# 64-byte tiles ahead of the weight buffers, and the small tiles at the other end of SBUF

## The chip, the cores and the metric

The kernel runs on one core of a Trainium2 chip. The metric is the device time of one execution in microseconds (us). Engines: PE is TensorE, DVE is VectorE, ACT is ScalarE, POOL is GpSimd, SP is SyncE. The on-chip memory SBUF has 128 partitions. A tile takes the same range of bytes in each of its partitions, so "address" below means the byte at which a tile starts in every partition, and "at 32" means that this address leaves 32 when divided by 128.

## What is computed

Two transformer blocks are chained on one sequence of 256 tokens of width 1024, in fp32. Cut to what carries the time:

```
h = rmsnorm(x, g_mix);  proj = h @ w_in              # block 1
o_swa, o_dsa, o_mem = three attentions on slices of proj
merged = sum of gate_i * (o_i @ w_proj_i)
x = x + merged @ w_out
x = x + square(relu(rmsnorm(x) @ w_mlp_in)) @ w_mlp_out
h = rmsnorm(x, g_final)
for layer in 0, 1:                                    # block 2
    h = post_norm(h, 0.5 * (silu(h @ w1) * (h @ w3)) @ w2)
    mix = sgu(h) if layer == 0 else nsa(h)            # gated MLP / sparse attention
    h = post_norm(h, mix)
    h = post_norm(h, 0.5 * (silu(h @ w1') * (h @ w3')) @ w2')
```

Every weight matrix is used once, on all 256 tokens.

## The kernel before

**Weights.** All weights are streamed from HBM in strips of 128 x 1024 floats. `Stream.load` puts one into one of five raw buffers `wr` (SP's queue). `Stream.prep` splits it: ACT copies it, rounded, into a `wh` buffer (L142), DVE subtracts to get the remainder in a `wl` buffer (L149). In block 1's mixers there are six pairs of `wh` and `wl`; once block 1's tiles are released, `Stream.add` brings three more pairs (pools `whi2` and `wlo2`), and the nine are used in turn. In the program's listing the first six `wh` are called wh_69 to wh_79 and the three added ones wh_1996, wh_1998 and wh_2000.

**Products.** Activations are split the same way, so one product is three matmuls (`mm3`, L273: hi x hi, hi x lo, lo x hi). A matmul has one operand that is loaded into the array first (its weight load is the PEld row of the profile) and one that streams through it, the moving one. Three shapes of use carry nearly all of the time:

- `up` (L284): a strip of weights is loaded, the transposed activations (256 columns of a `big` or `med` tile) move. One half strip is 24 matmuls.
- `down` (L304, matmuls at L311): the hidden activations in `t2` tiles are loaded, the weights move in 512 columns. Chunks of 24. `down_last` (L313) does the end of it through `mm3`, in parts of 512 and 256 columns.
- `row` (L294): activations in `big` are loaded, the weights move in 512 or 256 columns.

**Where tiles lie.** `run` opens the pools one after the other, and each begins where the one ahead of it ends: raw, whi, wlo, cp (constants, vectors, rotary tables), bp (eight `big` of 8192 bytes), mp (five `med` of 4096 bytes), sm (scalars for each row). `blocks` then opens b1 and t2 for block 1's mixers, releases them, and opens t2 with eleven tiles, whi2, wlo2 and p2 for the rest. What this gives in the built program:

| tiles | address before | mod 128 | address after | mod 128 |
|---|---|---|---|---|
| wr, 5 | 1152 | 0 | 1152 | 0 |
| wh and wl, first 6 pairs | 21632 to 70784 | 0 | 21696 to 70848 | 64 |
| `big`, 8 | 72032 | 96 | 72064 | 0 |
| `med`, 5 | 137568 | 96 | 137600 | 0 |
| t2, 7 (mixers) | 187072 | 64 | 158080 | 0 |
| t2, 11 (the rest) | 161696 | 32 | 158080 | 0 |
| wh and wl, 3 more pairs | 184224 to 208800 | 32 | 180672 to 205248 | 64 |

Every one of these tiles is a multiple of 512 bytes long and is cut in multiples of 512 bytes, so where an operand starts modulo 128 is where its tile starts. The order of work on each engine is set by the build's scheduler, except for what `pin` and `manual` fix.

Of the kernel before, what the change touches and what calls it, by code (L numbers as in the profile page):

```python
# [23 lines left out]
F32 = mybir.dt.float32  # L24
F32R = mybir.dt.float32r
I32 = mybir.dt.int32
# [150 lines left out]
class Ker:  # L177
# [7 lines left out]
    def run(self, stop=None):  # L185
        self.stop = stop
        with ExitStack() as es:
            P = lambda n, b=1, **k: es.enter_context(self.pool(n, b, **k))
            self.W = Stream(self.nc, P("raw"), P("whi"), P("wlo"), self.specs, self.pin)
            self.cp = P("cp")  # L190
            self.bp = P("bp", 8)
            self.mp = P("mp", 5)
            self.sm = P("sm", 6)
            self.ps = P("ps", 4, space=bass.MemoryType.PSUM)
            self.dp = P("dp", space=bass.MemoryType.DRAM)
            self.blocks()
        return self.W.specs
# [345 lines left out]

    def rope_tables(self, p, pos):
        nc = self.nc
        posf = p.tile([128, 2], F32, name="posf")
        self.pin(nc.vector.tensor_copy(posf, pos))
        r = p.tile([128, 2, 32], F32, name="ang")
        q = p.tile([128, 2, 32], F32, name="angq")
        for t in range(2):  # L550
            nc.vector.tensor_scalar(r[:, t], self.cst("inv"), posf[:, t:t + 1], None, op0=OP.mult)
        magic = 12582912.0
        nc.vector.tensor_scalar(q, r, 1.0 / (2 * math.pi), magic, op0=OP.mult, op1=OP.add)
        nc.vector.tensor_scalar(q, q, magic, None, op0=OP.subtract)
        c1 = 6.28125
        c2 = float((np.array(2 * math.pi - c1, np.float32).view(np.int32) & ~np.int32(0xfff)).view(np.float32))
        c3 = float(np.float32(2 * math.pi - c1 - c2))
        for c in (c1, c2, c3):
            nc.vector.scalar_tensor_tensor(r, q, -c, r, op0=OP.mult, op1=OP.add)
        pif = 3.1415925  # L560
        nc.vector.tensor_scalar(r, r, pif, -pif, op0=OP.min, op1=OP.max)
        cosT = p.tile([128, 2, 64], F32, name="cosT")
        sinT = p.tile([128, 2, 64], F32, name="sinT")
        nc.scalar.activation(sinT[:, :, 32:64], r, AF.Sin)
        nc.scalar.activation(q, r, AF.Abs)
        nc.vector.tensor_scalar(q, q, -1.0, math.pi / 2, op0=OP.mult, op1=OP.add)
        nc.scalar.activation(cosT[:, :, 0:32], q, AF.Sin)
        nc.vector.tensor_copy(cosT[:, :, 32:64], cosT[:, :, 0:32])
        nc.vector.tensor_scalar(sinT[:, :, 0:32], sinT[:, :, 32:64], -1.0, None, op0=OP.mult)
        return cosT, sinT  # L570
# [178 lines left out]
    def blocks(self):  # L749
        nc, I = self.nc, self.I  # L750
        with ExitStack() as es:
            p = es.enter_context(self.pool("b1"))
            self.tp = es.enter_context(self.pool("t2", 7))
            R, merge = self.mixers(p)
        es = ExitStack()
        with es:
            self.tp = es.enter_context(self.pool("t2", 11))
            self.W.add(es.enter_context(self.pool("whi2")), es.enter_context(self.pool("wlo2")), 3)
            self.p2 = es.enter_context(self.pool("p2"))
            self.chain(R, merge)  # L760
# [215 lines left out]
    def toeplitz(self):  # L976

        nc, I = self.nc, self.I
        rel = self.p2.tile([32, 16], F32, name="rel")
        nc.scalar.dma_start(rel, I["rel_table_2"])  # L980
        hot = self.med([128, 384])
        self.load_cst(("hot",), hot)
        ps = self.bank()
        nc.tensor.matmul(ps[:16, :384], rel, hot[:32], start=True, stop=True)
        f = self.med([16, 384])
        nc.vector.memset(f[:, 256:], BIG)
        nc.vector.tensor_scalar(f[:, :256], ps[:16, :256], -1.0, None, op0=OP.mult)
        scr = self.dp.tile([16, 384], F32, name="scr")
        nc.scalar.dma_start(scr, f)
        out = []  # L990
        for i in range(2):
            tp = self.big([128, 8, 256])
            if not self.dry:
                src = bass.AP(tensor=scr.tensor, offset=scr.offset + i * 8 * 384, ap=[[1, 128], [384, 8], [1, 256]])
                nc.scalar.dma_start(tp, src)
            out.append(tp)
        return out

    def kv_ffn(self, x, acc):
# [69 lines left out]
        def windows(slot):  # L1069
            T = Ts[slot]  # L1070
            flt = self.med([128, 16, 4, 15])
            if self.dry:
                src = Null()
            else:
                t0 = T[:]
                src = bass.AP(tensor=t0.tensor, offset=t0.offset, ap=[list(t0.ap[0]), [2, 16], [S, 4], [16, 15]])
            pes = pe[:, slot, :, None, None].to_broadcast([128, 16, 4, 15])
            nc.vector.tensor_add(flt, src, pes)
            f = flt.rearrange("p j g n -> p j (g n)")
            nc.vector.memset(fl[slot][:, :, 60:64].bitcast(F32), 0.0)  # L1080
            self.split(fl[slot][:, :, :60], fl[slot][:, :, 64:124], f)

        def compress():
            hid = []
            for s in range(2):
                w1 = I["cmp_w1_2"][s]
                ws = W.get(w1, 0, 8, 0, 256) + W.get(w1, 1024, 8, 0, 256)
                ps = self.bank()
                k = 0
                for wh, wl in ws:  # L1090
                    for i in range(4):
                        f = fl[s][:, k]
                        ops = [(124, wh), (60, wl)]
                        for m, w in ops[::-1] if k == 15 else ops:
                            nc.tensor.matmul(ps[:m, :256], f[:, :m], w[:, i], start=k == 0 and m == 124,
                                             stop=k == 15 and m == 124, skip_group_check=True)
                        k += 1
                r = self.t2([128, 256])
                nc.vector.tensor_copy(r[:124], ps[:124, :256])
                ps = self.bank()  # L1100
                h = self.p2.tile([128, 2, 60], F32, name=f"hid{s}")
                for f in range(2):
                    nc.tensor.matmul(ps[:, f * 60:(f + 1) * 60], r[:124, f * 128:(f + 1) * 128], self.two[:124, :60],
                                     start=True, stop=True)
                for f in range(2):
                    nc.scalar.activation(h[:, f], ps[:, f * 60:(f + 1) * 60], AF.Gelu, bias=self.col("cmp_b1_2", 2 * s + f))
                hid.append(h)
# [21 lines left out]
            for r in range(4):  # L1129
                rs = slice(32 * r, 32 * r + 32)  # L1130
                nc.vector.tensor_copy(self.vc[rs, :, r], ps[rs, :256].rearrange("p (g d) -> p g d", g=4))

        f = self.ffn(x, 1, 0, acc, {1: keys, 2: lambda: windows(0), 3: lambda: windows(1), 4: lambda: key(0), 5: compress, 6: lambda: key(1)})
        for _ in range(3):
            next(f)
# [163 lines left out]
    def mixers(self, p):  # L1299
# [5 lines left out]
        self.c, self.vec, self.vt = {}, {}, []  # L1305
        nc.sync.dma_start(R[:, 0], I["x"][0, :128])
        names = ("ident", "tril_t", "rowok")
        self.load_cst(names, self.cp.tile([128, 257], F32, name="cst"))
        self.ident = self.cst("ident")
        put = [self.vectors(("g_mix", "g_mem"), nc.scalar)]  # L1310
        nc.sync.dma_start(R[:, 1], I["x"][0, 128:])
# [1 line left out]
            for _ in range(4):  # L1313
                W.load()
        self.load_cst(("swa", "causal", "inv"), p.tile([128, 800], F32, name="cstp"))
        pos = p.tile([128, 2], I32, name="pos")
        nc.scalar.dma_start(pos, I["positions"].rearrange("o (t p) -> p (o t)", p=128))
        nr = [self.med([128, D]) for _ in range(2)]
        put.append(self.vectors(("b_gate", "cmp_b1_2"), nc.sync))
# [28 lines left out]
        W.pump()  # L1348
        mem = self.big([128, 2, D])
        nc.sync.dma_start(mem, I["mem"][0].rearrange("(t p) d -> p t d", p=128))  # L1350
        sink = p.tile([128, 8], F32, name="sink")
        nc.scalar.dma_start(sink, I["sinks"].to_broadcast([128, 8]))
        nsink = p.tile([128, 8], F32, name="nsink")
        self.pin(nc.vector.tensor_scalar(nsink, sink, -1.0, None, op0=OP.mult))
        self.cosT, self.sinT = self.rope_tables(p, pos)

# [35 lines left out]
        nc.scalar.copy(vd, PI[:, :, 64:128])  # L1392
        dup = p.tile([128, 2, 2, 64], F32, name="kidup")
        nc.scalar.copy(dup, Ri[:, :, None, 256:320].to_broadcast([128, 2, 2, 64]))
        wi = p.tile([128, 2, 4], F32, name="wi")
        nc.vector.tensor_scalar(wi, PI[:, :, 448:452], 1.0 / 16, None, op0=OP.mult)
        kd = p.tile([128, 2, 64], F32, name="kd")
        self.rope(PI, 0, 1, kd, self.med([128, 2, 64]))
# [184 lines left out]
```

## Time and profile before

| | us |
|---|---|
| time, median of three runs | 1486.18 |
| the three runs, lowest and highest | 1483.34, 1486.90 |
| the profiled execution's own time | 1484.42 |
| its span, first to last instruction | 1482.6 |

The profile is of one execution; the mean granted clock of the PE in it is 0.997 of full speed. A matmul's duration in the profile is the time from its start to a modelled end and overlaps the next one: most 256-column matmuls read 282 ns. What back-to-back matmuls take is read instead from the length of a stretch divided by the number of matmuls that start in it; below this is called the pitch. The count behind a stretch's busy time also takes in the one or two matmuls that run on into it.

### The profile page before, as it was taken

What the parts mean: (1) busy time and instruction counts of PE and PEld (TensorE: products, weight loads), DVE (VectorE), ACT (ScalarE), POOL (GpSimd) and SP (SyncE); (2) the same over time, 40 slices, a digit from 0 to 9 for tenths busy, and PEclk for the clock granted to TensorE, in tenths of its full rate; (3) what the DMA queues carried; (4) which work ended last, traced back from release to release, by engine and by line L of the source; (5) the groups of instructions that cost most, each with busy time, mean ns of one, the idle gap of its engine ahead of it and who ended that gap; (6) DMA issues with size and microseconds to landing.
All of it is one profiled execution on the core that took longest, in us unless ns stands there. A gap on an engine that the chain in (4) does not pass through costs nothing.

```text
span 1482.6 us, 25196 instructions
## 1 busy us (share of the span) xinstructions
PE 1443.6 (97%) x10093; PEld 1330.6 (90%) x10093; DVE 954.6 (64%) x1618; ACT 734.1 (50%) x1115; POOL 40.1 (3%) x49
## 2 busy tenths in 40 slices
PE   7899999999999999999999999999999999999997
PEld 6689998989999999889899999999999898899996
DVE  7884488555585455886685454874665778664544
ACT  5564565544354444454354444454654397354442
POOL 0000000000000000100010000100000121100001
PEclk9999999999999999999999999999999999999999
DMA  8453267756556666487546666467665452286650
GB/s 292 129 157 93 65 225 242 223 187 189 171 171 201 192 189 187 138 264 266 157 156 213 186 185 189 134 219 229 219 208 183 125 180 86 67 260 187 185 170 29
DMA packets 191714, 264.81 MB, mean 179 GB/s; under 512 B 11024, under 2 KB 159852, under 8 KB 191596
## 3 DMA queue, kind: packets, MB, share of 16 engines
q1 hardware_dynamic: 183068, 249.56, 53.7%
q10 hardware_dynamic: 8528, 13.64, 3.0%
q8 instruction: 79, 1.29, 0.3%
q14 instruction: 39, 0.32, 0.1%
HBM read 262.09 MB, written 1.07 MB: 177 GB/s over the span
## 4 chain that ended last, share of the span: by engine, by line
PE 83%; DVE 9%; ACT 3%; DMA 2%; issue 2%; DVEq 0%; ACTq 0%
PE acc L311 21%; PE u L275 17%; PE u L276 17%; PE u L277 17%; DVE wl L149 2%; PE acc L695 2%; PE acc L276 1%; PE acc L277 1%; PE acc L275 1%; ACT wh L142 1%; DVE big L850 1%; PE acc L681 1%; DVE bst L379 1%; DMA wr<-in_w_in_dram 1%; DVE big L828 1%
## 5 line engine op out<-in xcount | busy, mean ns | idle before, releaser
L149 DVE TENSOR_TENSOR wl<-wr,wh 128x1024 fp32r<-128x1024 f32 (+3 forms) x488 | 572.6, 1183 | 419.5 <-ACT wh L142 410.6
L142 ACT CAST wh<-wr 128x1024 fp32r<-128x1024 f32 (+3 forms) x488 | 493.3, 1019 | 536.3 <-PE u L276 231.2
L275 PE MATMUL u<-big,wh 128*128 128x256 f32 x1960 | 552.1, 282 | 1.6 <-ACT med L412 1.1
L277 PE MATMUL u<-big,wl 128*128 128x256 f32 x1960 | 550.3, 281 | 0.0
L276 PE MATMUL u<-big,wh 128*128 128x256 f32 x1960 | 550.2, 281 | 0.0
L275 PEld LDWEIGHTS u<-big,wh 128*128 128x128 f32 x1960 | 369.7, 189 | 4.7 <-ACT med L412 1.3
L276 PEld LDWEIGHTS u<-big,wh 128*128 128x128 f32 x1960 | 368.9, 188 | 2.1
L277 PEld LDWEIGHTS u<-big,wl 128*128 128x128 f32 x1960 | 369.6, 189 | 0.0
L311 PE MATMUL acc<-wh,t 128*128 128x512 f32 x928 | 264.0, 395 | 0.0
L311 PEld LDWEIGHTS acc<-wh,t 128*128 128x128 f32 x928 | 169.8, 188 | 35.0
L311 PE MATMUL acc<-wl,t 128*128 128x512 f32 x464 | 145.6, 394 | 0.0
L311 PEld LDWEIGHTS acc<-wl,t 128*128 128x128 f32 x464 | 87.2, 188 | 20.6
L275 PE MATMUL u<-wh,big 128*128 128x256 f32 (+1 forms) x304 | 100.8, 332 | 0.5 <-ACT t L1423 0.5
L277 PE MATMUL u<-wh,big 128*128 128x256 f32 (+1 forms) x304 | 100.5, 331 | 0.0
L276 PE MATMUL u<-wl,big 128*128 128x256 f32 (+1 forms) x304 | 100.0, 329 | 0.0
L331 ACT CAST t<-t 128x512 fp32r<-128x512 f32 x66 | 41.0, 621 | 56.6 <-DVE t L536 25.3
L275 PEld LDWEIGHTS u<-wh,big 128*128 128x128 f32 x304 | 57.1, 188 | 6.9 <-ACT t L1423 0.9
L277 PEld LDWEIGHTS u<-wh,big 128*128 128x128 f32 x304 | 57.1, 188 | 5.5
L276 PEld LDWEIGHTS u<-wl,big 128*128 128x128 f32 x304 | 57.1, 188 | 5.2
L836 POOL TENSOR_TENSOR big<-big,med 128x256 f32<-128x256 f32 x24 | 23.2, 985 | 1384.6 <-ACT big L835 1352.1
L332 DVE TENSOR_TENSOR t<-t,t 128x512 fp32r<-128x512 f32 x66 | 45.3, 686 | 15.1 <-ACT t L331 15.1
L276 PE MATMUL acc<-wl,t 128*128 128x512 f32 (+1 forms) x168 | 53.9, 321 | 0.3 <-DVE wl L149 0.3
(256 smaller groups left out, 1344.3 us busy)
## 6 DMA issues: line engine op xcount, KB each, us to landing
wr<-in_ffn_w_dram SPq DMA_DIRECT2D x264, 512.0 KB, 4.4
wr<-in_w_in_dram SPq DMA_DIRECT2D x34, 512.0 KB, 4.5
wr<-in_w_mlp_in_dram SPq DMA_DIRECT2D x32, 512.0 KB, 4.6
wr<-in_w_mlp_out_dram SPq DMA_DIRECT2D x32, 512.0 KB, 3.9
wr<-in_sgu_w_in_dram SPq DMA_DIRECT2D x32, 512.0 KB, 5.3
wr<-in_sgu_w_out_dram SPq DMA_DIRECT2D x16, 512.0 KB, 5.5
wr<-in_kv_w_dram SPq DMA_DIRECT2D x12, 512.0 KB, 4.4
wr<-in_w_out_dram SPq DMA_DIRECT2D x8, 512.0 KB, 3.8
```

Of the source, the lines that this page charges most:

```text
L142: self.nc.scalar.copy(h, v)
L149: self.nc.vector.tensor_sub(l, v, h.bitcast(F32))
L275: mm(out, lh, rh, start=start, stop=False, **k)
L276: mm(out, lh, rl, start=False, stop=False, **k)
L277: mm(out, ll, rh, start=False, stop=stop, **k)
L311: mm(acc[t][n], a[:, k, ts], b[:, 0, n * 512:(n + 1) * 512], start=s, stop=e)
L331: self.nc.scalar.copy(h, x)
L332: return self.nc.vector.tensor_sub(l, x, h.bitcast(F32))
L379: b = nc.vector.bn_stats(st[:, 6 * i:6 * i + 6], x[:, c0:c1])
L681: nc.tensor.transpose(pt[:, c:c + 128], e[:, c:c + 128], self.ident)
L695: nc.tensor.matmul(out, PT[:, c:c + 128], v(b), start=b == 0, stop=b == nb - 1)
L836: nc.gpsimd.tensor_mul(x[:, cs], x[:, cs], gB[:, cs])
```

## The change

The pools are laid out anew, with nothing else edited in what is computed. A pool `sa` with one tile of 64 bytes (the positions as floats) stands between raw and whi, `sb` with one of 64 bytes (the sinks) behind wlo, and `sc` with one of 64 bytes (`rel`, the relative bias table) ahead of whi2. cp and sm are put at the other end of SBUF (`side="right"`), t2 of the mixers comes ahead of b1, and two tiles are padded (the constants from 257 to 288 floats, `hid` from 60 to 64 columns). The table above has the addresses. Before, the starts of the loaded and of the moving operand differed by 96 or 64 modulo 128 in `up`, by 32 or 64 in `row`, by 96 or 0 in `down`; after, weights start at 64 and activations at 0 in all three, in both parts of the program.

```diff
--- before.py
+++ after.py
@@ -186,11 +186,16 @@
         self.stop = stop
         with ExitStack() as es:
             P = lambda n, b=1, **k: es.enter_context(self.pool(n, b, **k))
-            self.W = Stream(self.nc, P("raw"), P("whi"), P("wlo"), self.specs, self.pin)
-            self.cp = P("cp")
+            raw, self.sa = P("raw"), P("sa")
+            posf = self.sa.tile([128, 16], F32, name="posf")
+            self.W = Stream(self.nc, raw, P("whi"), P("wlo"), self.specs, self.pin)
+            self.sb = P("sb")
+            self.posf, self.sink = posf, self.sb.tile([128, 16], F32, name="sink")
+            self.kp = P("kp")
+            self.cp = P("cp", side="right")
             self.bp = P("bp", 8)
             self.mp = P("mp", 5)
-            self.sm = P("sm", 6)
+            self.sm = P("sm", 6, side="right")
             self.ps = P("ps", 4, space=bass.MemoryType.PSUM)
             self.dp = P("dp", space=bass.MemoryType.DRAM)
             self.blocks()
@@ -543,7 +548,7 @@
 
     def rope_tables(self, p, pos):
         nc = self.nc
-        posf = p.tile([128, 2], F32, name="posf")
+        posf = self.posf[:, :2]
         self.pin(nc.vector.tensor_copy(posf, pos))
         r = p.tile([128, 2, 32], F32, name="ang")
         q = p.tile([128, 2, 32], F32, name="angq")
@@ -749,12 +754,13 @@
     def blocks(self):
         nc, I = self.nc, self.I
         with ExitStack() as es:
+            self.tp = es.enter_context(self.pool("t2", 7))
             p = es.enter_context(self.pool("b1"))
-            self.tp = es.enter_context(self.pool("t2", 7))
             R, merge = self.mixers(p)
         es = ExitStack()
         with es:
             self.tp = es.enter_context(self.pool("t2", 11))
+            self.rel = es.enter_context(self.pool("sc")).tile([128, 16], F32, name="rel")
             self.W.add(es.enter_context(self.pool("whi2")), es.enter_context(self.pool("wlo2")), 3)
             self.p2 = es.enter_context(self.pool("p2"))
             self.chain(R, merge)
@@ -976,7 +982,7 @@
     def toeplitz(self):
 
         nc, I = self.nc, self.I
-        rel = self.p2.tile([32, 16], F32, name="rel")
+        rel = self.rel[:32]
         nc.scalar.dma_start(rel, I["rel_table_2"])
         hot = self.med([128, 384])
         self.load_cst(("hot",), hot)
@@ -1098,7 +1104,7 @@
                 r = self.t2([128, 256])
                 nc.vector.tensor_copy(r[:124], ps[:124, :256])
                 ps = self.bank()
-                h = self.p2.tile([128, 2, 60], F32, name=f"hid{s}")
+                h = self.p2.tile([128, 2, 64], F32, name=f"hid{s}")[:, :, :60]
                 for f in range(2):
                     nc.tensor.matmul(ps[:, f * 60:(f + 1) * 60], r[:124, f * 128:(f + 1) * 128], self.two[:124, :60],
                                      start=True, stop=True)
@@ -1305,7 +1311,7 @@
         self.c, self.vec, self.vt = {}, {}, []
         nc.sync.dma_start(R[:, 0], I["x"][0, :128])
         names = ("ident", "tril_t", "rowok")
-        self.load_cst(names, self.cp.tile([128, 257], F32, name="cst"))
+        self.load_cst(names, self.kp.tile([128, 288], F32, name="cst"))
         self.ident = self.cst("ident")
         put = [self.vectors(("g_mix", "g_mem"), nc.scalar)]
         nc.sync.dma_start(R[:, 1], I["x"][0, 128:])
@@ -1313,7 +1319,7 @@
             for _ in range(4):
                 W.load()
         self.load_cst(("swa", "causal", "inv"), p.tile([128, 800], F32, name="cstp"))
-        pos = p.tile([128, 2], I32, name="pos")
+        pos = self.cp.tile([128, 2], I32, name="pos")
         nc.scalar.dma_start(pos, I["positions"].rearrange("o (t p) -> p (o t)", p=128))
         nr = [self.med([128, D]) for _ in range(2)]
         put.append(self.vectors(("b_gate", "cmp_b1_2"), nc.sync))
@@ -1348,9 +1354,9 @@
         W.pump()
         mem = self.big([128, 2, D])
         nc.sync.dma_start(mem, I["mem"][0].rearrange("(t p) d -> p t d", p=128))
-        sink = p.tile([128, 8], F32, name="sink")
+        sink = self.sink[:, :8]
         nc.scalar.dma_start(sink, I["sinks"].to_broadcast([128, 8]))
-        nsink = p.tile([128, 8], F32, name="nsink")
+        nsink = self.cp.tile([128, 8], F32, name="nsink")
         self.pin(nc.vector.tensor_scalar(nsink, sink, -1.0, None, op0=OP.mult))
         self.cosT, self.sinT = self.rope_tables(p, pos)
 
@@ -1392,7 +1398,7 @@
         nc.scalar.copy(vd, PI[:, :, 64:128])
         dup = p.tile([128, 2, 2, 64], F32, name="kidup")
         nc.scalar.copy(dup, Ri[:, :, None, 256:320].to_broadcast([128, 2, 2, 64]))
-        wi = p.tile([128, 2, 4], F32, name="wi")
+        wi = self.cp.tile([128, 2, 4], F32, name="wi")
         nc.vector.tensor_scalar(wi, PI[:, :, 448:452], 1.0 / 16, None, op0=OP.mult)
         kd = p.tile([128, 2, 64], F32, name="kd")
         self.rope(PI, 0, 1, kd, self.med([128, 2, 64]))
```

PE, POOL and SP run the same rows in the same order as before. On ACT the DMA that fetches the table `rel` (32 x 16 floats) stands at another place. Before, at the program's start, ahead of the first cast of a weight strip:

```order
L267 COPY vt_111<-u 128x16
L980 DMA rel<-in_rel_table_dram 32x16
L142 CAST wh_69<-wr_64 128x904
L142 CAST wh_71<-wr_65 128x904
L412 ACTIVATE med<-u,vt_111 128x128 x4
```

After, the first cast follows the copy, and the DMA is issued some 130 rows later, where the added buffers are first filled:

```order
L142 CAST wh_2009<-wr_72 128x256
L142 CAST wh_2011<-wr_68 128x256
L1540 ACTIVATE big<-big 128x512
L732 CAST med<-u 128x2x128
L142 CAST wh_2013<-wr_69 128x256
L986 DMA rel<-in_rel_table_dram 32x16
L142 CAST wh_81<-wr_72 128x512
L142 CAST wh_83<-wr_68 128x256
```

(wh_2009, wh_2011 and wh_2013 are the three added buffers there, wh_73 to wh_83 the first six.) The same place on ACT before:

```order
L727 CAST med<-u 128x2x128
L142 CAST wh_1996<-wr_68 128x256
L142 CAST wh_1998<-wr_64 128x256
L1534 ACTIVATE big<-big 128x512
L142 CAST wh_2000<-wr_65 128x256
L142 CAST wh_77<-wr_68 128x512
```

So besides the DMA, the last cast of an attention output (L727, L732 after; `rows_T`) has moved behind two casts of weights and one sigmoid step, and its partner on DVE behind the matching subtractions.

## Rows read from the trace of the kernel before

**Rows 1.** The page: busy time and share of each engine; granted clock in 40 slices.

```profile
PE 1443.6 (97%) x10093; PEld 1330.6 (90%) x10093; DVE 954.6 (64%) x1618; ACT 734.1 (50%) x1115; POOL 40.1 (3%) x49
PEclk9999999999999999999999999999999999999999
```

**Rows 2.** Stretch, length; busy (x) of PE, PEld, DVE, ACT, POOL; clock, DMA, GB/s.

```profile
205.00:250.00 45.00, 44.66 (x254) 37.30 (x253) 41.32 (x75) 24.85 (x34) 0.00 (x0) 1.00 0.69 234
250.00:430.00 180.00, 179.56 (x1174) 163.27 (x1173) 111.33 (x141) 85.41 (x102) 0.00 (x0) 1.00 0.59 186
430.00:600.00 170.00, 170.00 (x1215) 159.67 (x1215) 91.94 (x98) 75.43 (x83) 2.05 (x2) 1.00 0.63 195
```

**Rows 3.** Waits: who waited for whom, us in total, times, longest.

```profile
DVE wl L149 <- ACT wh L142: 410.6, 271, 5.4
ACT wh L142 <- PE u L276: 231.2, 168, 4.8
ACT wh L142 <- PE acc L311: 140.3, 98, 8.8
...
PE u L266 <- DMA med<-in_g_mem_dram: 6.3, 1, 6.3
```

**Rows 4.** Groups by line and form, whole span: count, busy, mean ns of one.

```profile
L149 DVE TENSOR_TENSOR wl<-wr,wh 128x1024 fp32r<-128x1024 f32 x458 | 556.3, 1223 | 405.6 <-ACT wh L142 396.7 <-PE u L276 6.6
L275 PE MATMUL u<-big,wh 128*128 128x256 f32 x1952 | 549.9, 282 | 1.6 <-ACT med L412 1.1 <-DVE nm L671 0.5
L142 ACT CAST wh<-wr 128x1024 fp32r<-128x1024 f32 x458 | 478.2, 1051 | 520.7 <-PE u L276 222.6 <-PE acc L311 140.3 <-issue 97.2
L311 PE MATMUL acc<-wh,t 128*128 128x512 f32 x928 | 264.0, 395 | 0.0
L311 PE MATMUL acc<-wl,t 128*128 128x512 f32 x464 | 145.6, 394 | 0.0
L275 PE MATMUL u<-wh,big 128*128 128x512 f32 x128 | 51.2, 400 | 0.5 <-ACT t L1423 0.5
L275 PE MATMUL u<-wh,big 128*128 128x256 f32 x176 | 49.6, 282 | 0.0
```

**Rows 5.** Stretches of `up` (128x256, `big` moving); columns as in Rows 2.

```profile
434.44:439.88 5.44, 5.44 (x50) 5.44 (x49) 4.27 (x4) 4.18 (x5) 0.00 (x0) 1.00 0.97 355
445.47:456.83 11.36, 11.36 (x97) 11.35 (x96) 5.04 (x5) 4.70 (x5) 0.00 (x0) 1.00 0.75 231
484.89:490.54 5.65, 5.65 (x50) 5.65 (x49) 2.45 (x3) 2.60 (x3) 0.00 (x0) 1.00 0.61 187
```

**Rows 6.** Chain of work, 428 to 510 us: start, length, `down` chunks of 24.

```profile
440.05 5.59 PE acc L311 x24
456.99 5.44 PE acc L311 x24
473.78 5.60 PE acc L311 x24
```

**Rows 7.** Stretches of `row` (weights moving), then of `down_last`; columns as in Rows 2.

```profile
622.44:623.84 1.40, 1.40 (x7) 1.12 (x6) 1.30 (x2) 0.00 (x0) 0.00 (x0) 1.00 0.98 342
640.57:643.32 2.75, 2.75 (x14) 2.25 (x12) 2.52 (x3) 2.33 (x4) 0.00 (x0) 1.00 0.97 306
757.23:758.59 1.36, 1.36 (x14) 1.36 (x13) 0.71 (x2) 1.36 (x3) 0.00 (x0) 1.00 0.00 0
759.96:762.76 2.80, 2.80 (x26) 2.80 (x25) 2.00 (x3) 2.79 (x5) 0.00 (x0) 1.00 0.69 204
232.26:232.98 0.72, 0.72 (x9) 0.72 (x7) 0.72 (x2) 0.00 (x0) 0.00 (x0) 1.00 0.35 114
```

**Rows 8.** Timeline of ACT: start, length, work, [idle before and its releaser].

```profile
6.62 0.33 ACTq L980 DMA_DIRECT2D rel<-in_rel_table_dram  x1
8.38 0.94 ACT L142 CAST wh<-wr 128x904 fp32r<-128x904 f32 x1 [1.59 <-DMA wr<-in_w_in_dram]
...
179.80 0.37 ACT L727 CAST med<-u 128x256 fp32r<-128x256 f32 x1 [0.85 <-PE u L724]
180.07 0.71 ACT L142 CAST wh<-wr 128x256 fp32r<-128x256 f32 x2
180.69 0.63 ACT L1534 ACTIVATE big<-big 128x512 f32<-128x512 f32 x1
181.22 0.39 ACT L142 CAST wh<-wr 128x256 fp32r<-128x256 f32 x1
183.65 0.62 ACT L142 CAST wh<-wr 128x512 fp32r<-128x512 f32 x1 [2.04 <-DMA wr<-in_w_proj_swa_dram]
```

## The prediction

> **What bounds the kernel now.** I read the page first: the PE is busy for 97% of the span, DVE for 64%, ACT for 50%, at a granted clock of 0.9 or more in every slice [rows 1] and 1.00 in the stages read here. Then the stages: through the long feed-forward stretches the PE has next to no gap, 179.56 of 180 us and 170.00 of 170, while DVE stands at 62% and 54% and the DMA engines at about 0.6 [rows 2]. The waits say the same from the other side. ACT's casts wait for the PE to give a weight buffer back (231 and 140 us), DVE's subtractions wait for the casts (411 us), and the PE's own largest wait is 6.3 us, once, at the start [rows 3]. So the time is the sum of what the matmuls take one after another, and a change that moves no work can change it only through that, or through a new gap.
>
> The grouped rows say that a 256-column matmul lasts 282 ns and a 512-column one some 395 to 400 [rows 4]. These are pipelined durations and don't sum to the span; what counts is the pitch, and it isn't the same everywhere. In `up`, 96 matmuls with weights in the first six buffers take 11.36 us, 118.3 ns each; 48 with weights in the three added buffers take 5.44 us, 113.3 ns; and 48 on the very same added buffers, 50 us later, take 5.65 us, 117.7 ns [rows 5]. In `down`, a chunk of 24 takes 5.59 or 5.60 us (233 ns) on the first six and 5.44 us (226.7 ns) on the added ones, a chunk with both in between [rows 6]. In `row` at 512 columns it is 1.40 us for six, 233.3 ns, on a buffer of the first six and 2.75 us for twelve, 229.2 ns, on added ones; at 256 columns 2.80 us for 24, 116.7 ns, against 1.36 us for twelve, 113.3 ns [rows 7]. Clock and shape are equal in these pairs, and the DMA share is not what tells them apart: 0.97 in the quickest stretch of `up`, 0.75 and 0.61 in the slower ones [rows 5]. What differs is which buffer is read, and with it the start modulo 128 of the two operands.
>
> Sorting all 6,060 matmuls of `up` by buffer, with their starts taken in order from the trace: the 4,242 on the first six (weights at 0, activations at 96) keep the 118.3 of the 445 us stretch throughout. The 1,818 on the added ones (at 32 and 96) have two levels, as the two short stretches show. 666 of them lie in half strips at about 113.3, 1,152 in half strips at about 117.8; the mean is 0.37 x 113.3 + 0.63 x 117.8 = 116.2. A level, once taken, mostly lasts until other buffers come.
>
> **The change, part by part.** The first part is the starts. After it, weights start at 64 and activations at 0, a difference of 64 for every pair. Today 64 is the difference of `up` and `row` on the added buffers, which is the better class of both, so I price the change by giving those pitches to all.
>
> - `up`, first six: 4,242 x (118.3 - 116.2) = 8.9 us less. Bounds: 0 (nothing moves) and 4,242 x 5.0 = 21.2 us (all at 113.3). I take the mean of the added buffers, since it has the new difference; that all would be at the lower level has only a third of that class for it.
> - `up`, added: difference 64 before and after, 0. Bounds: 1,818 x 2.9 = 5.3 us less, 1,818 x 2.1 = 3.8 us more.
> - `down`, first six, 1,038 matmuls at 512 columns with a difference of 96: no `down` of today has 64, so it takes the pitch of `row` at 64, 229.2 [rows 7]: 1,038 x (233.3 - 229.2) = 4.3 us less. Bounds 0 and 1,038 x 6.6 = 6.9 us.
> - `down`, added, 522 matmuls: difference 0 becomes 64. Their mean today is 228.8 (226.7 at best, [rows 6], more where a chunk mixes both kinds), so 522 x 0.4 = 0.2 us more. Bounds 1.1 less, 522 x 4.5 = 2.3 more.
> - `row` on the first six: 324 at 512 columns x 4.1 = 1.3 us less; 504 at 256 columns. Their new pitch is the mean of the 136 on added buffers, 115.9 (the 113.3 of rows 7 is their lower level): 504 x 0.8 = 0.4 us less. Bounds 0 and 2.1 + 1.7 us.
> - `down_last` at 256 columns, 335 matmuls at some 118.5: with both operands at 32 it reads 0.72 us for six, 120.0 [rows 7]. Taken as 0, bounds 1.7 less, 0.5 more.
>
> These lie on the path: back-to-back PE work ends each of these stretches, and the strips that feed it have slack (ACT's casts wait for the PE to free a buffer). The one stretch where that is thin is 205 to 250 us, with DVE at 41.3 of 45 us; there at most 0.5 us of the gain could turn into a wait.
>
> The second part is the moved rows. The DMA of `rel` takes 0.33 us of ACT's queue at 6.62 us, and the cast behind it waits until 8.38 us for its strip anyway [rows 8]: nothing is gained by its leaving. At its new place the same 0.33 us stands ahead of casts that wait 2.04 us for a strip at 183.65 us, so nothing is lost. The delayed cast L727 stands behind 0.71 us of casts and a 0.63 us sigmoid step; its result goes to a projection whose strip comes later. I take 0, bounds 0 and 1 us more. The third part, small tiles at the far end and padding, changes where ACT and DVE read. Their large rows show a single duration for all buffers, 1,223 and 1,051 ns a strip [rows 4], and both engines have slack: 0.
>
> Sum: 8.9 + 4.3 - 0.2 + 1.3 + 0.4 = 14.7 us. The profiled execution's 1484.42 would become 1469.7; the median of the runs is 1.8 us above it, so 1486.2 - 14.7 = 1471.5.
>
> **A rule weighed.** The rows show 113.3 to 118.3 ns at 256 columns, depending on buffers [rows 5]. The Trainium skill, "TensorE: Matmul & The Clock Gate", section "Step-by-step: what each phase is for", says that the PE reads moving operand and weights through two independent ports, and that loading the next weights doesn't steal bandwidth from the running matmul; addresses don't appear in it. By that rule this change does nothing, which is the second rival below. The trace doesn't settle it outright, but a pitch that differs by 4% with the same shape and clock speaks against it.
>
> **The rivals.**
>
> 1. All pairs at the lower level. If starts at 0 and 64 let every matmul run at 113.3 or 226.7, the bounds add up: 21.2 + 5.3 + 6.9 + 1.1 + 2.4 (`row`, 512) + 2.1 (`row`, 256) + 1.7 = 40.7 us, giving 1445. For it: every start then leaves 0 or 64, and in none of today's pairs do both (activations are at 96 or 32), so today's two levels may be what a start at 32 costs; and a lower level lasts once taken, with no buffer of the first kind left to break it. Against it: difference 64 today gives the upper level more often, and 512-column `row` at 64 has 229.2, not 226.7.
> 2. The start modulo 128 isn't the cause, but the region of SBUF (the first six lie at 21 to 71 KB, the added ones at 184 to 209 KB) or the order of work. Then nothing moves: 1486. For it: in today's trace start and region always change together. Against it: the same added buffers read two levels.
> 3. Slower: the pairs never take the lower level. Then `up` on the added buffers rises to 118.3 (3.8 us), `down` there to 233.3 (2.3 us), `row` at 512 by 132 x 4.1 = 0.5 us and at 256 by 0.1 us: 6.7 us more, 1493. For it: difference 0, which gives `down` its 226.7, exists no longer, and the upper level is the commoner one at 64. It decides as soon as `up` on the first six stays above 118.0. The worst pitch of the trace, 120.0 for all of `up` [rows 7], would add 4,242 x 1.7 + 1,818 x 3.8 = 14.1 us in place of the 3.8, 1503.
>
> **How the numbers follow.** A measurement of this kernel can tell about 0.3% (4.5 us) from no change. My forecast, a mixture of levels as today's difference of 64 shows it: 0.43. Rival 1: 0.24. Rival 2: 0.18. Rival 3: 0.15. The first two are faster by more than 0.3%, so faster 0.67, same 0.18, slower 0.15. The predicted time is the forecast's, 1471. Its own range, from half the sum to one and a half times it (7 to 22 us less), is 1464 to 1479. The range for all reaches from rival 1, 1445, to 1490, so that it leaves out most of rival 3 (0.12) and the far end of rival 1 (0.04).
>
> **What would show it.** Right: `up` on the first six buffers between 113.3 and 118 ns, with half strips at two levels; chunks of `down` near 5.5 us in place of 5.60; PE still at 97%, and all stages shorter by about 1% alike. Rival 1 shows 48 matmuls of `up` in 5.44 us everywhere. Rival 2 shows 11.36 and 5.60 unchanged. Rival 3 shows no stretch of `up` at 5.44 for 48 any more. The forecast is wrong too if a new wait of the PE shows near 184 us, or if casts and subtractions change their durations with the new addresses.

## The result and the profile after

The changed kernel takes 1461.81 us (median of four runs, 1461.58 to 1463.18) against 1484.91 us for the kernel before on the same chip: a ratio of 0.9846, 95% interval 0.9829 to 0.9863, or 23.1 us less. The prediction said 1471, in a range of 1445 to 1490; its forecast alone said 1464 to 1479.

The page of the changed kernel has nearly the same shares as [rows 1], with the PE still the engine that is always busy; its busy time fell by 23.8 us.

```profile
PE 1419.8 (97%) x10093; PEld 1311.5 (90%) x10093; DVE 955.1 (65%) x1618; ACT 733.8 (50%) x1115; POOL 40.2 (3%) x49
```

The waits, answering to [rows 3]: ACT and DVE wait for the same things as before, in these two rows 20 and 24 us less in all, as they would if the PE gives buffers back sooner.

```profile
DVE wl L149 <- ACT wh L142: 386.4, 213, 5.1
ACT wh L142 <- PE u L281: 211.3, 167, 3.8
```

The same three stretches of `up` as in [rows 5], found by the number of their first matmul (line numbers are higher by 5 or 6 after the change): 48 matmuls on two of the added buffers, 96 on four of the first six, 48 on the two added buffers again. Columns as in [rows 2].

```profile
431.02:436.68 5.66, 5.66 (x51) 5.66 (x50) 4.37 (x4) 4.30 (x5) 0.00 (x0) 1.00 1.01 355
442.28:453.18 10.90, 10.90 (x98) 10.90 (x96) 4.98 (x5) 4.70 (x5) 0.00 (x0) 1.00 0.70 209
480.54:485.98 5.44, 5.44 (x51) 5.44 (x49) 2.45 (x3) 2.60 (x3) 0.00 (x0) 1.00 0.70 204
```

The middle one is the gain: 10.90 for 11.36 us, 113.5 ns a matmul for 118.3. The other two changed places. The stretch that had 113.3 has 117.8 now, and the one that had 117.7 has 113.3: the two levels are still there, and what matters is how often each is taken. Over all 6,060 matmuls of `up`, half strips at the lower level hold 5,212 now; before it was 666.

The chunks of `down`, in the chain of work, answering to [rows 6]:

```profile
436.84 5.60 PE acc L316 x24
453.34 5.49 PE acc L316 x24
469.74 5.49 PE acc L316 x24
```

The first of them still takes 233 ns a matmul, the others 229, on the first six and on added buffers alike. The first is the one that follows the stretch of `up` at 117.8 ns shown above; the 39 chunks of 24 with `up` at the lower level on both sides all take 229. And `row`, answering to [rows 7]: six matmuls of 512 columns on the first six, twelve on added buffers, and twelve of 256 columns on an added one.

```profile
614.65:616.02 1.37, 1.37 (x7) 1.13 (x6) 1.37 (x2) 0.00 (x0) 0.00 (x0) 1.00 1.01 336
632.50:635.25 2.75, 2.75 (x14) 2.25 (x12) 2.42 (x3) 1.35 (x2) 0.00 (x0) 1.00 0.97 317
739.46:740.88 1.42, 1.42 (x15) 1.42 (x13) 1.42 (x6) 0.00 (x0) 0.00 (x0) 1.00 0.00 0
```

512 columns went from 233.3 to 229 ns on the first six; the 256-column stretch on an added buffer, 113.3 before, has 117.8 now (twelve matmuls in 1.414 us by their starts; the stretch shown ends a little later).

Strip by strip, the casts and subtractions last what they did in [rows 4]:

```profile
L149 DVE TENSOR_TENSOR wl<-wr,wh 128x1024 fp32r<-128x1024 f32 x458 | 556.9, 1224 | 383.6 <-ACT wh L142 372.8 <-PE u L282 0.2
L142 ACT CAST wh<-wr 128x1024 fp32r<-128x1024 f32 x458 | 477.7, 1050 | 492.3 <-PE u L281 200.0 <-PE acc L316 132.7 <-issue 96.1
```

Since both kernels run the same matmuls in the same order, the time from each one's start to the next can be subtracted one by one. In us, after minus before: `up` on the first six -18.6, on the added ones -3.8; `down` (with the 512-column part of `down_last`) -4.2 and -0.1; `row` +0.3; `down_last` at 256 columns 0.0; all else +3.9. The sum is -22.3.

### The profile page after: what moved, and what is told of

Its sections match the earlier page's. It is cut to its first block, busy times and chain, and to the rows that moved or that the text cites. A ratio compares the mean times of both kernels' runs of the same rounds, so it can differ in the third digit from the quotient of the medians.

```text
span 1460.1 us, 25195 instructions
## 1 busy us (share of the span) xinstructions
PE 1419.8 (97%) x10093; PEld 1311.5 (90%) x10093; DVE 955.1 (65%) x1618; ACT 733.8 (50%) x1115; POOL 40.2 (3%) x49
## 4 chain that ended last, share of the span: by engine, by line
PE 82%; DVE 11%; ACT 3%; DMA 2%; issue 2%; DVEq 0%; ACTq 0%; SPq 0%
PE acc L316 21%; PE u L280 17%; PE u L281 17%; PE u L282 17%; DVE wl L149 2%; PE acc L700 2%; PE acc L281 1%; PE acc L282 1%; PE acc L280 1%; ACT wh L142 1%; DVE bst L384 1%; DVE big L856 1%; PE acc L686 1%; DVE big L834 1%; PE u L805 1%
## 5 line engine op out<-in xcount | busy, mean ns | idle before, releaser
L280 PE MATMUL u<-big,wh 128*128 128x256 f32 x1960 | 545.2, 278 | 1.6 <-ACT med L417 1.1
L281 PE MATMUL u<-big,wh 128*128 128x256 f32 x1960 | 542.9, 277 | 0.0
L282 PE MATMUL u<-big,wl 128*128 128x256 f32 x1960 | 542.8, 277 | 0.0
```

The lines of the kernel that those rows point to most:

```text
L280: mm(out, lh, rh, start=start, stop=False, **k)
L281: mm(out, lh, rl, start=False, stop=False, **k)
L282: mm(out, ll, rh, start=False, stop=stop, **k)
```

## The experiments

In all of them, call d the start of the weights minus the start of the activations. The section on the change counted the moving operand's start minus the loaded one's; for `up` that is the other way round, so `up` on the first six buffers of the kernel before, 96 modulo 128 there, has d = 32. Each kernel differs from the changed one in the lengths of the small tiles ahead of the pools, or in one more small tile there, and no more (e9 differs from the kernel before), and all run the same matmuls in the same order. Not all cuts are multiples of 512 bytes: the strips of 904 columns are cut at 452, or 1,808 bytes, so 18 of 6,072 matmuls of `up` and half of the 48 of 452 columns have other starts; the 6,060 leave out 12 of those 18. The kernel before, run beside each experiment for its ratio, had medians of 1485.6 to 1485.9 us. To compare them I show the same 96 matmuls of `up` on the first six buffers in each, 11.36 us before and 10.90 after. Means of pitches below leave out those of over 122.7 ns (256 columns) and 245 ns (512 columns). The longest of these hold a wait, but at d = 32 and 128 most are matmuls of 123 to 130 ns, so `up` reads 0.2 to 0.4 ns too low there: the 118.3 of the kernel before reads 118.0.

**e1: the new layout with the old starts.**

```diff
-            posf = self.sa.tile([128, 16], F32, name="posf")
+            posf = self.sa.tile([128, 32], F32, name="posf")
-            ... self.sb.tile([128, 16], F32, name="sink")
+            ... self.sb.tile([128, 24], F32, name="sink")
+            es.enter_context(self.pool("tq")).tile([128, 16], F32, name="tq")    # ahead of each t2
-            self.rel = es.enter_context(self.pool("sc")).tile([128, 16], F32, name="rel")
+            self.rel = es.enter_context(self.pool("sc")).tile([128, 32], F32, name="rel")
```

> The changed kernel's layout (small tiles at the far end, the moved DMA of rel, t2 ahead of b1) with the starts modulo 128 of the kernel before: weights of the first six buffers at 0, big and med at 96, t2 and the added buffers at 32. Theory A (the starts modulo 128 make the whole difference): the time of before, about 1485 us, up on the first six at 118.3 ns. Rival R (the region of SBUF or the moved rows make it): the changed kernel's time, about 1462 us.

Measured: 1489.64 us, ratio to before 1.0028 (1.0019 to 1.0038). The stretch of 96 is back at the old length:

```profile
446.92:458.28 11.36, 11.36 (x98) 11.36 (x96) 5.04 (x5) 4.70 (x5) 0.00 (x0) 1.00 0.75 234
```

So theory A holds for the gain: neither the place of the small tiles, nor the region, nor the moved rows bring any of it. It is even 4 us slower than the kernel before, with the same starts modulo 128. By subtraction of the traces, `up` on the added buffers takes 2.4 us more and their 512-column `down` 0.9 us; why these changed comes out with e4.

**e2 and e3: other starts, the same difference.** In e2 `posf` has 40 floats in place of 16: weights at 32, activations at 96. In e3 it has 32: weights at 0, activations at 64.

> All weights start at 32, all activations at 96: the difference is 64 for every pair as in the changed kernel, but no start leaves 0 or 64. Theory A1 (only the difference of the two starts counts): same as the changed kernel, 1462 us within 3, up mostly at 113.3 ns, down at 229 ns. Theory A2 (a start must also be a multiple of 64): up takes the lower level no more often than the added buffers of before did, a third, so 1468 to 1476 us.

> Weights and activations change places: weights start at 0, activations at 64. Theory A1 and A2 (difference 64, both multiples of 64): 1462 us within 3. If it matters which of the two operands is at 64, the up pitch on all buffers differs from the changed kernel's 114.1 ns mean; by 2 ns that would be 12 us, 1474 us or more.

Measured: e2 1460.79 us, 0.9832 (0.9815 to 0.9848); e3 1459.26 us, 0.9821 (0.9779 to 0.9862). The stretch of 96 in e2, then in e3:

```profile
440.10:451.00 10.90, 10.90 (x97) 10.89 (x96) 4.98 (x5) 4.70 (x5) 0.00 (x0) 1.00 0.82 266
```

```profile
441.82:452.73 10.91, 10.91 (x98) 10.91 (x96) 5.01 (x5) 4.70 (x5) 0.00 (x0) 1.00 0.76 242
```

A1 it is, not A2: both kernels are where the changed one is. A multiple of 64 is of no importance in itself, only the difference of the starts.

**e4: difference 0 modulo 128.** `posf`, `sink` and `rel` have 32 floats each.

> All weights and all activations start at 0, a difference of 0. Theory A1 (a difference of 64 is what helps): down falls from 229.1 to 226.7 ns, its pitch at difference 0 before (1560 x 2.4 = 3.7 us less), and up rises to 117.8 ns or more, which it kept in the kernel before behind every chunk of down (6060 x 3.7 = 22 us more): about 1480 us. Theory A3 (multiples of 64 are enough, whatever the difference): 1458 to 1462 us.

Measured: 1493.33 us, 1.0045 (1.0031 to 1.0059): slower than the kernel before. The stretch of 96 takes 120 ns a matmul:

```profile
446.53:458.04 11.51, 11.51 (x97) 11.51 (x96) 5.10 (x5) 4.69 (x5) 0.00 (x0) 1.00 0.85 273
```

A3 falls. A1 is right in `up`, which loses more than I had put, and wrong in a detail: `down` was to have 226.7 ns on all buffers, and had a mean of 228.2 on the first six, 232.2 on the added ones. Both are at 0 modulo 128. They differ modulo 256: d is 0 for the first six and 128 for the added ones. The kernels before and after have d = 64 modulo 256 wherever it is 64 modulo 128, but in e1 the added buffers had 192 (and 128 in `down`, where the kernel before has 0), and there `up` read 117.5 and `row` 232.9 ns. So the next four set d modulo 256, alike for all pairs.

**e5 to e8: d = 192, 128, 0 and 96 modulo 256.** `posf` has 32 floats in each; `sink` has 48, 64, 32 and 8, `rel` 48, 32, 64 and 24.

> Weight start minus activation start is 192 modulo 256 for every pair of both sets of buffers (64 modulo 128, as in the changed kernel, where it is 64 modulo 256). Theory P128 (the starts count modulo 128): as the changed kernel, 1461 us, up mostly at 113.3 ns. Theory P256 (they count modulo 256): the added buffers of the first experiment had 192 and read 117.5 ns in up and 232.9 ns at 512 columns, so 6060 x 3.4 + 2016 x 3.7 = 28 us more than 1462: about 1490 us.

> Weight start minus activation start is 128 modulo 256 for every pair. P128: the same as a difference of 0, so like the next kernel. P256: up at 118.6 and 512 columns at 232.3 ns, as the added buffers of the fourth experiment read at 128: 1462 + 6060 x 4.5 + 2016 x 3.1 = 1495 us.

> Weight start minus activation start is 0 modulo 256 for every pair (the fourth experiment had 0 for the first six buffers and 128 for the added ones). P128: nothing changes against that one, 1493 us, 512 columns at two pitches. P256: up at 119.8 everywhere, 512 columns at 228.1: 1462 + 6060 x 5.7 - 2016 x 1.0 = 1495 us, with no 512-column chunk near 232 ns left.

> Weight start minus activation start is 96 modulo 256 for every pair, which no large group of matmuls had yet. If a difference of 64 is a single good point: up between 117 and 120 ns as at 0, 32, 128 and 192, 1485 to 1495 us. If good differences form a band about 64: up near 114 ns, 1462 us.

Measured: e5 1486.55 us, 1.0017 (1.0006 to 1.0028); e6 1493.82, 1.0064 (1.0044 to 1.0083); e7 1492.43, 1.0062 (1.0041 to 1.0083); e8 1488.98, 1.0020 (1.0009 to 1.0031). The stretch of 96 in e5, e6, e7 and e8, in this order:

```profile
446.81:458.12 11.31, 11.31 (x98) 11.30 (x96) 5.04 (x5) 4.69 (x5) 0.00 (x0) 1.00 0.72 232
```

```profile
447.59:458.98 11.39, 11.39 (x97) 11.39 (x96) 5.05 (x5) 4.69 (x5) 0.00 (x0) 1.00 0.68 203
```

```profile
446.70:458.21 11.51, 11.51 (x97) 11.51 (x96) 5.10 (x5) 4.69 (x5) 0.00 (x0) 1.00 0.73 225
```

```profile
447.16:458.55 11.39, 11.39 (x97) 11.39 (x96) 5.05 (x5) 4.69 (x5) 0.00 (x0) 1.00 0.77 240
```

e5 is the one that decides: 64 modulo 128 as in the changed kernel, 192 modulo 256, and the whole gain is gone. P128 falls. In e7 the 512-column matmuls, at two pitches in e4, are all near 228, as P256 had it. The chain's chunks of `down` in e5 and in e7, two of each:

```profile
441.37 5.60 PE acc L316 x24
458.28 5.60 PE acc L316 x24
```

```profile
441.40 5.47 PE acc L316 x24
458.38 5.47 PE acc L316 x24
```

At 96 there is no band about 64 either, on this grid of 32 bytes. Finer steps were not tried, nor d = 160 or 224 for all pairs.

**e9: padding alone.** The kernel before with

```diff
-        self.load_cst(names, self.cp.tile([128, 257], F32, name="cst"))
+        self.load_cst(names, self.cp.tile([128, 313], F32, name="cst"))
+            es.enter_context(self.pool("q1")).tile([128, 40], F32, name="q1")    # ahead of t2, mixers
+            es.enter_context(self.pool("q2")).tile([128, 48], F32, name="q2")    # ahead of t2, the rest
+            es.enter_context(self.pool("q3")).tile([128, 16], F32, name="q3")    # ahead of whi2
```

> The kernel before with four paddings and nothing else (the constants' tile 257 to 313 floats, 160 bytes ahead of t2 in the mixers, 192 bytes ahead of t2 and 64 bytes ahead of the added buffers in the rest): small tiles and the DMA of rel stay where they were, weight start minus activation start becomes 64 modulo 256 everywhere. If that difference makes the whole gain: 1461 us within 3, as the changed kernel. If moving the small tiles or the DMA has a share: above 1464.

Measured: 1461.46 us, 0.9829 (0.9812 to 0.9845).

```profile
441.79:452.69 10.90, 10.90 (x97) 10.90 (x96) 4.98 (x5) 4.70 (x5) 0.00 (x0) 1.00 0.75 236
```

The whole gain, with the small tiles and the DMA where they were.

**e10: does `down` set the level of the next `up`?** `posf` 32 and `rel` 64 floats, and a tile of 16 floats ahead of each t2: d stays 64 for `big` and `med` and becomes 0 for t2.

> The difference of weights and big or med stays 64 modulo 256 (up and row), that of weights and t2 becomes 0 (down and down_last), whose pitch at 512 columns was 227.9 ns against 229.1. Theory O (each matmul's pitch follows from its own pair): up stays at 114.1, down gains 1560 x 1.2 = 1.9 us, down_last loses 335 x 3.7 = 1.2 us: 1461 us. Theory H (up takes over the level in which the chunk of down ahead of it leaves the PE; behind down at difference 0 it was the upper one 45 of 45 times in the kernel before): up at 117.8, 6060 x 3.7 = 22 us more, about 1482 us.

Measured: 1473.94 us, 0.9926 (0.9909 to 0.9943). Three stretches in a row: 48 matmuls of `up`, a chunk of `down`, 96 of `up`.

```profile
430.83:436.27 5.44, 5.44 (x50) 5.44 (x49) 3.75 (x4) 4.19 (x5) 0.00 (x0) 1.00 0.97 354
436.27:441.73 5.46, 5.46 (x26) 4.52 (x25) 4.02 (x6) 3.11 (x4) 0.00 (x0) 1.00 0.93 288
441.73:453.04 11.31, 11.31 (x98) 11.31 (x96) 5.08 (x5) 4.69 (x5) 0.00 (x0) 1.00 0.77 234
```

This is theory H, seen at one place: `up` at 113.3 ns, a quicker `down`, and then `up` at 117.8 with the same d as ahead of the chunk (on other buffers). Behind `down` the upper level came 45 of 45 times. In the changed kernel it is 4 of 45, and in e2, e3 and e9, where d is 64 for all pairs too, 4 of 45 each: in the other 41 the first three to five matmuls behind the chunk still take about 117 to 124 ns, and the rest 113.3.

Theory H gave 45 of 45 for the kernel before, behind `down` at difference 0. That count was wrong: 28 of the 45 stand ahead of `up` on the first six (d = 32), which never takes the lower level anyway. The 17 that tell something stand ahead of the added buffers, 16 behind `down` at d = 0 and one at 224; all 17 are at the upper level.

The size was off (1482 expected), since `up` in stretches without `down` still reached the lower level: its mean is 116.7 ns. By the means, 6060 x (116.7 - 114.1) - 1560 x (229.1 - 227.1) = 12.6 us more than the changed kernel, against 12.1 measured.

**e11: the added buffers at d = 32.** `posf` 32 and `rel` 72 floats.

> The first six weight buffers keep a difference of 64 modulo 256, the three added ones get 32 (the two classes of the kernel before, exchanged). Theory O: up on the first six stays at 114.1, on the added ones it goes to 118.0 and their down to 233.2: 1818 x 3.9 + 522 x 4.1 = 9 us more, 1470 us. Theory H: the strips at 32 also push the first six out of the lower level, which then hold it a third of the time as the added ones did before, 116.2: 4242 x 2.1 = 9 us more again, 1479 us.

Measured: 1471.83 us, 0.9905 (0.9885 to 0.9925). The 96 on the first six, and the 48 on two added buffers ahead of them:

```profile
444.59:455.50 10.91, 10.91 (x98) 10.90 (x96) 5.01 (x5) 4.71 (x5) 0.00 (x0) 1.00 0.73 234
433.42:439.10 5.68, 5.68 (x51) 5.68 (x50) 3.56 (x4) 3.95 (x5) 0.00 (x0) 1.00 0.97 346
```

Here theory O has it: the first six keep a mean of 113.9 ns although strips at d = 32 run between theirs, and the added ones go to 118.0. So not every pair with another d takes the lower level away. In this program `down` on the first six is nearly always followed by `up` on the first six; that `down` has d = 64 here, and behind it `up` was at the lower level 27 of 27 times.

## Why the prediction was right, and which step was off

The mechanism was the one that I forecast: the starts of the two operands set the pitch, and the PE's pitch is the time. The sum, 14.7 us, was too small by 8.4 us: 1461.8 lies in the stated range, but outside the forecast's own 1464 to 1479, on the side of rival 1. Term by term, against the subtraction of the two traces:

- `up` on the first six: 8.9 us forecast, 18.6 measured. This is the term that was mis-sized. I took 116.2 ns, the mean of the added buffers, on the ground that they had the new difference and held the lower level a third of the time. The third wasn't a property of that difference: in the kernel before, `down` had a d of 0 or 224 modulo 256, and behind it `up` on the added buffers began at the upper level 17 of 17 times. The change sets d to 64 for `down` too, which ends that (e10 takes it back and loses 12 of the 23 us). The trace of before had it: each of those 17 groups was at the upper level, and I wrote that a level lasts.
- `up` on the added ones: 0 forecast, 3.8 less measured, within the bound of 5.3, for the same reason.
- `down`: 4.3 less and 0.2 more forecast, 4.2 less and 0.1 less measured. Pricing it by `row` at the same difference, 229.2, was right: its mean is 229.1.
- `row`: 1.7 us less forecast, 0.3 more measured. The 512-column pitch fell as put, but six matmuls of `row` early in block 1 took 427 ns each, at a granted clock of 0.50, the lower level (1.2 GHz), which followed 20.3 us of which the PE was busy for 18.4. The kernel before has such a drop of the clock too, at 151 us, under other matmuls. `Row` at 256 columns stayed at 116.8 ns on average.

```profile
43.10:45.40 2.30, 2.30 (x7) 1.82 (x6) 1.19 (x1) 1.08 (x2) 0.00 (x0) 0.50 0.98 303
```

- The moved rows: 0 forecast. The DMA of `rel` is issued at 180.47 us now, and no new wait of the PE shows there; e9, which doesn't move it, is as quick.

Rival 1 asked for starts that are multiples of 64; e2 has none and is as quick, so its reason was wrong, though 5,212 of 6,060 matmuls did reach its level. Rival 2 falls with e1. The Trainium skill, "TensorE: Matmul & The Clock Gate", section "Step-by-step: what each phase is for", says that loading the next tile's weights takes no read bandwidth from the running matmul. I had taken that to mean that addresses change nothing, and the runs don't agree: at one clock and shape, the mean pitch of `up` goes from 114.1 (d = 64) to 119.9 ns (d = 0) with d alone, though they don't show that it is the weight load that costs the time. Rival 3 was a real danger, if not of these starts: e4, e6 and e7 are 7 to 8 us slower than the kernel before.

One assumption of mine was wrong without costing anything. I counted starts modulo 128. By e5 they count modulo 256, and the new kernel happened to be at 64 in both. That was luck: at 192, which is 64 modulo 128 as well, the time is that of before.

The first matmuls of this profile come later than before (the 41st at 23.1 us for 19.9), and the two are level again at 205 us. Thirteen matmuls of 452 columns start 376 ns apart on average, where the same ones took 205 before; two of them, after and then before:

```profile
19.81 0.58 PE L281 MATMUL acc<-wl,big 128*128 128x452 f32 x1
20.19 0.58 PE L282 MATMUL acc<-wh,big 128*128 128x452 f32 x1
17.54 0.37 PE L276 MATMUL acc<-wl,big 128*128 128x452 f32 x1
17.74 0.36 PE L277 MATMUL acc<-wh,big 128*128 128x452 f32 x1
```

452 columns in 376 ns are 1.2 a ns, as at the lower clock level, 1.2 GHz; the trace's clock record begins at 21.9 us, at full clock, and at 14.8 us before. Until 16.25 us the PE had waited now and then (0.95 and 0.70 us the last times), from there on it ran without a gap, and from 21.9 us on these matmuls take 205 ns here too. That is 2.2 of the 3.9 us of "all else". All eleven experiments have 6 to 14 such slow matmuls at the start, e1 with the old starts 8 and e9 with paddings alone 12. With one profile of the kernel before, it isn't shown whether the layout has a part in it.

## What to carry to other kernels

Where the PE is the bound and its matmuls run back to back, divide the length of a stretch by its matmuls, by buffer: if one shape has several pitches at one clock, look at the start addresses of its two operands, for here a few paddings, and nothing else, were worth 1.6%. Judge a start by the pair, not by its own alignment, and price the matmuls that run ahead of it as well: a pair that is the best for one shape (d = 0 for `down`) can cost more in the next one than it gives.

## What the runs showed of the hardware

At full clock, the pitch of these fp32r matmuls (128 x 128 loaded) depends on d, the start of the weights minus the start of the activations, modulo 256: e2 and e3 moved both operands' starts with d kept, which changed nothing, and e5 moves the activations alone, by 128 bytes against e3 (the added buffers by 256), which takes the whole gain. Mean pitches in ns:

| d modulo 256 | `up`, 256 columns | `down`, 512 columns | kernel with all pairs at d, us |
|---|---|---|---|
| 0 | 119.9 (e7) | 227.9 (e7) | 1492.4 |
| 32 | 118.0 (before) | 232.7 (e11) | not run |
| 64 | 114.1 (after) | 229.1 (after) | 1461.8 |
| 96 | 117.9 (e8) | 233.2 (e8) | 1489.0 |
| 128 | 118.6 (e6) | 232.3 (e6) | 1493.8 |
| 192 | 117.6 (e5) | 233.3 (e5) | 1486.6 |
| 224 | not run | 233.4 (before) | not run |

That the period is 256 and not 512 can be seen in the changed kernel itself: by the addresses, d modulo 512 is 320 for `big` with the first six buffers and 64 with the added ones, and both have a mean of 114.1 ns. d isn't counted by role: the weights are the loaded operand in `up` and the moving one in `down`, so each column holds for its own shape.

At d = 64, `up` has two levels, 113.3 and 117.8 ns, and holds the one it is in: in the changed kernel's trace, a group of `up` on one pair of buffers (mostly twelve matmuls) that directly followed another had, by its median, the same level all 464 times, 406 times the lower and 58 times the upper. There, a level changed only where other work stood between. What sets it was only tested for `down`. Why d matters isn't shown by any of these runs: they don't tell a slower weight load from a slower moving operand.
